# A Strassen-Winograd MLP kernel: one more nested product, accumulating stores and a new order of the weight sums

## The chip, the cores and the metric

The kernel runs on one core of one Trainium2 chip. The metric is device time in microseconds (us), the median of several executions. Executions of the kernel before agree within 0.2%. Engines are named as in the profile: PE is TensorE (matmul), DVE is VectorE, ACT is ScalarE, POOL is GpSimd, SP is SyncE, which issues most DMAs (in the kernel before 454 of 594 plain ones and all 54 transposes). bX, bY, bZ, bW and bT are the banks that PE writes its results into.

## The reference

```python
batch, m, k, h, n = 16, 512, 768, 3072, 768      # all float32

def reference(x, w1, b1, w2):
    y = np.matmul(x, w1) + b1
    y = 0.5 * y * (1.0 + erf(y / np.sqrt(2.0)))
    return np.matmul(y, w2)
```

The rows of x are handled in eight blocks of 1024. Each block has a first product (x with W1, then GELU) and a second product (with W2).

## The kernel before

Matmuls run in fp16 with fp32 accumulation. Both products use the Strassen-Winograd scheme: sums of blocks on DVE, then 7 block products instead of 8. Some of the seven W2 products go one level deeper and are again done as 7 instead of 8; I call these **nested**. Later blocks nest all seven; blocks 0 and 1 nest only some, and do the rest in plain **row units** (128 rows at a time, 12 matmuls of 384 columns for one product). Which ones are nested is one table of (block, product):

```python
HYBRID = ((0, 2), (1, 1), (1, 4), (1, 2))
```

A nested product needs sums of quarters of its W2 operand. They are made once by DVE in a few **staging buffers**, stored to a DRAM scratch `w2s` by SP, and loaded again where they are used:

```python
def split_w2(p, t, q=None):
    b11, b12, b21, b22 = quarters(p)
    def put(q, src, eng=nc.sync):
        eng.dma_start(out=w2s[p, q][:], in_=src)
    t = {n: spare[k] for n, k in zip((7, 5, 6, 4), t)}       # t: four staging buffers
    for n, a, b in ((7, b22, b12), (5, b12, b11), (6, b22, t[5]), (4, b21, t[6])):
        def f(n=n, a=a, b=b):
            tt(t[n], a, b, SUB)                              # DVE
            puts.append([LAG[0], lambda eng: put(n, t[n], eng)])   # stored LAG slots later, by SP
        later(WB, f, slow if q is None else q)
```

LAG is 2, and 3 in block 1's last row units. A sum that writes a staging buffer must wait until the last store out of that buffer has landed. In the kernel before, the order was: products 6, 1, 4, 2 in block 0's row units, 7 and 5 in the nested units of block 1 (buffers 6 to 9), and 3 in block 1's last row units (buffers 1 to 4).

The program places all side work in numbered slots of a unit's period. In block 0's first product two of these placements matter here:

```python
if slot == (1 if pos < at[1, 0] else 4) and pos + 1 < len(seq) and seq[pos + 1][0] == 0:
    prep_wt(seq[pos + 1][1])                 # DVE sums of the next W1 tile
if slot == 4:
    ...
    if pos == at[1, 0] - 2:
        x_sums(1, soon, slice(0, RH // 2), (0, 1))    # first-half sums of block 1's x
```

At the very start PE runs matmuls whose result nobody reads, while the inputs load (`spin(9)`, then four times `spin(2)`):

```python
def spin(n):
    for k in range(n):
        nc.tensor.matmul(out=(bX[1], bY[1])[k % 2][:], lhsT=zero[:, 0, 0:P], rhs=zero[:, 0, :],
                         start=True, stop=True, skip_group_check=True)
```

## Time and profile before

| | before |
|---|---|
| time, median of 3 | 852.22 us (851.93 to 852.35) |
| span of the profiled execution | 850.3 us |
| PE busy, matmuls | 843.9 us (99%), 6468 |
| last matmul starts | 846.31 us |
| from there to the end | 4.03 us |

PE is the bound and has hardly a gap. The list of PE's waits (engine, bank and line, released by; then us in total, times, longest) holds only the start-up:

```profile
PE bX L756 <- DVE arena L742: 1.2, 1, 1.2
PE bT L330 <- DVE arena L762: 1.1, 2, 0.9
```

The DMA view of the kernel before for 178 to 195 us (out<-in, issuing queue, count, size each, median us from issue to landing) shows stores of W2 sums landing far later than in a quiet stretch (3.9 us for those of 118 to 180 us):

```profile
w2s<-arena SPq DMA_DIRECT2D x5, 288.0 KB, 7.7
arena<-in_x_dram POOLq DMA_DIRECT2D x5, 192.0 KB, 7.9
```

### The profile page before, as it was taken

To read this page: it belongs to the slowest core of one execution; us is meant where nothing else is said; L and a number is where in the kernel's file an instruction comes from. 1 tells how busy PE (TensorE), PEld (TensorE's weight loads), DVE (VectorE), ACT (ScalarE), POOL (GpSimd) and SP (SyncE) were. 2 spreads that over 40 slices of the span, in tenths; PEclk is the share of its full clock that TensorE was granted. 3 is DMA by queue.
4 is the path that set the end of the run, shared out by engine and by line. 5 is a ranking of instruction groups with operands and counts; after the bars stand their busy time and mean duration, and the time that the engine had idled before them with its cause. 6 is when DMAs were issued, how large, how long until landed. Compare 5 with 4: busy or idle time off the path is not lost.

```text
span 850.3 us, 16583 instructions
## 1 busy us (share of the span) xinstructions
PE 843.9 (99%) x6468; PEld 571.3 (67%) x6468; DVE 671.1 (79%) x1132; ACT 423.6 (50%) x692; POOL 89.9 (11%) x147
## 2 busy tenths in 40 slices
PE   8999999999999999999999999999999999999998
PEld 5444445697544897449964499645995469944798
DVE  5766679877757998679976799667996689956998
ACT  4777762221277413773147822587216771277611
POOL 5021100022200002000020000200002100010000
PEclk9999999999999999999999999999999999999999
DMA  9998697679899699977999689995999949984398
GB/s 226 193 281 182 159 194 256 232 203 262 314 278 207 199 336 363 307 166 246 337 372 283 134 287 335 373 286 112 314 345 349 293 102 331 354 312 170 101 303 290
DMA packets 144066, 220.82 MB, mean 260 GB/s; under 512 B 61916, under 2 KB 84884, under 8 KB 143988
## 3 DMA queue, kind: packets, MB, share of 16 engines
q1 hardware_dynamic: 117536, 178.36, 67.0%
q0 software_dynamic: 26272, 41.30, 21.7%
q8 instruction: 50, 0.82, 0.4%
q14 instruction: 28, 0.23, 0.1%
q10 hardware_dynamic: 180, 0.11, 0.0%
HBM read 182.07 MB, written 47.87 MB: 270 GB/s over the span
## 4 chain that ended last, share of the span: by engine, by line
PE 98%; DMA 1%; ACT 0%; DVE 0%; SPq 0%; issue 0%; ACTq 0%
PE bY L411 21%; PE bY L516 15%; PE bX L411 14%; PE bX L516 10%; PE bW L411 7%; PE bZ L411 7%; PE bZ L516 5%; PE bW L516 5%; PE bY L456 5%; PE bZ L456 2%; PE bW L456 2%; PE bY L603 1%; PE bX L603 1%; PE bX L456 1%; DMA arena<-in_x_dram 1%; PE bX L778 0%
## 5 line engine op out<-in xcount | busy, mean ns | idle before, releaser
L208 DVE TENSOR_TENSOR arena<-arena 128x1536 f16<-128x1536 f16 (+6 forms) x634 | 405.9, 671 | 6.6 <-PE bW L456 1.0
L411 PEld LDWEIGHTS <-arena 128*128 128x128 f16 x1974 | 192.5, 98 | 224.3 <-issue 0.6
L516 PEld LDWEIGHTS <-arena 128*128 128x128 f16 x3528 | 292.1, 98 | 8.3 <-issue 0.4
L411 PE MATMUL bY<-arena 128*128 128x512 f16 x846 | 214.4, 379 | 0.1
L629 DVE TENSOR_TENSOR arena<-bY,arena 128x512 f32<-128x512 f32 (+1 forms) x102 | 69.4, 680 | 119.0 <-PE bY L411 91.9
L516 PE MATMUL bY<-arena 128*128 128x192 f16 x1500 | 138.3, 246 | 0.0
L411 PE MATMUL bX<-arena 128*128 128x512 f16 x564 | 138.2, 379 | 0.0
L622 ACT COPY bY<-bX 128x512 f32<-128x512 f32 (+1 forms) x144 | 79.1, 549 | 118.2 <-DVE arena L565 81.5
L427 ACT ACTIVATE arena<-arena,b1t 128x1024 f16<-128x1024 f32 x94 | 108.0, 1149 | 52.0 <-DVE arena L657 52.0
L642 ACT COPY arena<-bW 128x512 f32<-128x512 f32 (+1 forms) x148 | 81.5, 551 | 92.2 <-PE bW L516 44.3
L516 PE MATMUL bX<-arena 128*128 128x192 f16 x1020 | 93.1, 246 | 0.1
L657 DVE TENSOR_TENSOR arena<-bZ,arena 128x512 f32<-128x512 f32 (+1 forms) x102 | 69.2, 679 | 22.1 <-PE bZ L411 18.2
L411 PE MATMUL bZ<-arena 128*128 128x512 f16 x282 | 76.2, 379 | 0.0
L411 PE MATMUL bW<-arena 128*128 128x512 f16 x282 | 76.2, 379 | 0.0
L548 POOL DMA_DIRECT2D out_dram<-arena x42 | 30.5, 728 | 409.1 <-DVE arena L653 375.0
L432 ACT ACTIVATE arena<-bX,b1t 128x512 f16<-128x512 f32 x94 | 64.0, 681 | 10.5 <-PE bX L411 10.5
L673 ACT COPY bZ<-bY 128x512 f32<-128x512 f32 (+1 forms) x58 | 30.8, 532 | 75.6 <-PE bY L456 30.0
L456 PEld LDWEIGHTS <-arena 128*128 128x128 f16 x480 | 46.9, 98 | 31.0 <-issue 0.2
L432 ACT ACTIVATE arena<-bY,b1t 128x512 f16<-128x512 f32 x94 | 63.4, 674 | 0.0
L516 PE MATMUL bZ<-arena 128*128 128x192 f16 x504 | 48.5, 246 | 0.0
L516 PE MATMUL bW<-arena 128*128 128x192 f16 x504 | 48.4, 246 | 0.0
L316 POOL DMA_DIRECT2D arena<-in_x_dram x60 | 32.3, 546 | 152.3 <-DMA arena<-arena 142.0
(62 smaller groups left out, 413.9 us busy)
## 6 DMA issues: line engine op xcount, KB each, us to landing
arena<-w2s SPq DMA_DIRECT2D x300, 288.0 KB, 4.6
arena<-w1s SPq DMA_DIRECT2D x72, 672.0 KB, 7.0
out_dram<-arena POOLq DMA_DIRECT2D x46, 384.0 KB, 7.4
w2s<-arena SPq DMA_DIRECT2D x49, 288.0 KB, 4.1
arena<-in_x_dram POOLq DMA_DIRECT2D x60, 192.0 KB, 7.3
w1s<-arena SPq DMA_DIRECT2D x12, 672.0 KB, 6.1
arena<-in_w_dram POOLq DMA_DIRECT2D x17, 384.0 KB, 7.5
out_dram<-arena SPq DMA_DIRECT2D x9, 384.0 KB, 2.6
```

The source lines that it names most:

```text
L208: nc.vector.tensor_tensor(out=o, in0=a, in1=b, op=op)
L316: nc.gpsimd.dma_start(out=xhs[t], in_=xr[:, sb * 8 + t, :])
L411: nc.tensor.matmul(out=dst[:, 0:RH], lhsT=w1_op(self.wt, slot)[:, c, :], rhs=a[:, c, :], start=first and c == 0, stop=c == self.C - 1, ski ...
L427: nc.scalar.activation(out=self.G[1][:, hi, :, :], in_=self.tmp, func=GELU, bias=b1t[:, 2 * hi + 1:2 * hi + 2])
L432: nc.scalar.activation(out=self.G[0][:, hi, row, :], in_=bank[:, 0:RH], func=GELU, bias=b1t[:, 2 * hi:2 * hi + 1])
L456: nc.tensor.matmul(out=dst[:, 0:N2], lhsT=a, rhs=w[:, :, c, :], start=first and c == 0, stop=c == self.C - 1, skip_group_check=True)
L516: nc.tensor.matmul(out=dst[:, t * N4:(t + 1) * N4], lhsT=a, rhs=w[:, c, :], start=first and c == 0 and t == ts[0], stop=c == NQ - 1, skip_ ...
L622: nc.scalar.copy(out=bY[u.g % 2][:, 0:u.F], in_=bX[u.g % 2][:, 0:u.F])
L629: nc.vector.tensor_tensor(out=u.c22(), in0=bY[u.g % 2][:, 0:u.F], in1=w[:, 0:u.F], op=ADD)
L642: nc.scalar.copy(out=w[:, 0:u.F], in_=bW[:, 0:u.F])
L657: nc.vector.tensor_tensor(out=u.c12(), in0=bZ[:, 0:u.F], in1=w[:, 0:u.F], op=ADD)
L673: nc.scalar.copy(out=bZ[:, 0:u.F], in_=bY[u.g % 2][:, 0:u.F])
```

## The change

The intent: nest product 4 of block 0 too (fewer matmuls), let DMA add the results of block 0's products 2 and 4 into the output in memory instead of DVE and ACT, and move the sums of W1 tile 6 so that a bank is emptied in time. To make room, the W2 sums get a new order. The core of the diff:

```diff
-        HYBRID = ((0, 2), (1, 1), (1, 4), (1, 2))
+        HYBRID = ((0, 2), (0, 4), (1, 4), (1, 1), (1, 2))
...
             def finish(self):
-                if self.p == 2:
-                    for n in range(NU):
-                        nc.gpsimd.dma_start(out=orr[...], in_=self.dst[:, n // 2, n % 2])
+                if self.sb and self.p != 2:
+                    return
+                for n in range(NU):
+                    ...
+                    if self.sb:
+                        nc.gpsimd.dma_start(out=o, in_=d)
+                    else:
+                        nc.gpsimd.dma_start(out=o, in_=d, accum_op=ADD)
...
-            if slot == (1 if pos < at[1, 0] else 4) and pos + 1 < len(seq) and seq[pos + 1][0] == 0:
+            if slot == (1 if pos < at[1, 0] - 2 else 4) and pos + 1 < len(seq) and seq[pos + 1][0] == 0:
                 prep_wt(seq[pos + 1][1])
...
-                    for p, t in ((6, (0, 1, 2, 3)), (1, (4, 5, 0, 1)), (4, (2, 3, 4, 5)), (2, (0, 1, 2, 5))):
-                        split_w2(p, t)
+                    w4 = (6, 4, 5, 3)
+                    split_w2(4, w4, ns=(5, 6, 4))
+                    split_w2(1, (0, 1, 2, 6))
+                    split_w2(2, (3, 0, 1, 2))
+                    split_w2(4, w4, ns=(7,))
...
-                split_w2(7, (6, 7, 8, 9))
-                split_w2(5, (6, 7, 8, 9))
+            if m == 2 and slot == 5:
+                for p in (6, 7):
+                    split_w2(p, (7, 8, 9, 10))
...
             if k == 0 and slot == 4:
                 LAG[0] = 3
-                split_w2(3, (1, 2, 3, 4))
+                for p in (5, 3):
+                    split_w2(p, (0, 2, 3, 5))
```

Cut: the new places of buffers and level sums, full-row stores of block 0, and the changed slots of the W2 loads.

More of the change, by code (lines that the diff above doesn't have):

```diff
@@ L152 @@
     tmps1 = [tmp_at(o_tmp + 4 * k * RH) for k in range(2)]
-    o_stage = o_wt + 2 * N + PAR
+    o_stage = o_wt + PAR
     stage = [cut(o_stage + k * WB, WB, "p (c n) -> p c n", c=NQ)
@@ L164 @@
           for o in (o_x0 + W2_N, o_x0 + W2_N + GS_N, o_x1, o_x1 + GS_N)]
-    osbs = [[cut(o, n).bitcast(FP32) for o, n in zip(oo, (2 * N2, 2 * N))]
-            for oo in ((o_x1 + 2 * GS_N + 2 * N + 2 * N2, o_wt),
-                       (o_x1 + 2 * GS_N + 2 * N, o_x1 + 2 * GS_N))]
-    assert 2 * N + 4 * N2 <= PAR
-    par02, par1, par4 = [cut(o, PAR).bitcast(FP32).rearrange(
-        "p (r t h n) -> p r t h n", r=2, t=2, h=2) for o in (o_wt + 2 * N, 2 * XT_N, o_x1 + 2 * GS_N)]
+    osbs = [[cut(o + a * 2 * N, 2 * N).bitcast(FP32) for a in range(2)]
+            for o in (o_wt, o_x1 + 2 * GS_N)]
+    par02, par04, par1, par4 = [cut(o, PAR).bitcast(FP32).rearrange(
+        "p (r t h n) -> p r t h n", r=2, t=2, h=2)
+        for o in (o_wt, o_x1, 2 * XT_N, o_x1 + 2 * GS_N)]
     par11 = cut(o_w2, W2P).bitcast(FP32).rearrange("p (c n) -> p c n", c=NH)[:, 0:8, 0:N4].rearrange(
@@ L180, in wb_at @@
         return cut(off, WB, "p (c n) -> p c n", c=NQ)
-    hyb_lev = [[strip(0, 0, 0, 0), strip(1, 1, 0, 0), Gs[0][1][:, 0:NQ, 0, 2 * P:RH], strip(1, 1, NQ, 0)],
-               [strip(0, 1, 0, 0), strip(0, 0, NQ, 0), strip(0, 1, NQ, 0), strip(0, 0, 0, 2 * P)],
-               [strip(0, 1, 0, 2 * P), strip(0, 0, NQ, 2 * P), strip(0, 1, NQ, 2 * P), strip(0, 0, 0, 0)],
-               [strip(0, 1, 0, 0), strip(0, 0, NQ, 0), strip(0, 1, NQ, 0), strip(0, 0, NQ, 2 * P)]]
+    S = [strip(0, a, c, r) for r in (0, 2 * P) for c in (0, NQ) for a in range(2)]
+    hyb_lev = [[S[0], S[1], Gs[0][1][:, 0:NQ, 0, 2 * P:RH], S[2]],
+               [S[3], S[4], Gs[0][1][:, 0:NQ, 1, 2 * P:RH], S[6]],
+               [S[5], S[7], S[0], S[1]],
+               [S[2], S[3], S[4], S[6]],
+               [S[5], S[0], S[7], S[2]]]
     spare = stage + [wb_at(2 * XT_N + o) for o in
@@ L189 @@
     assert XT_N + 2 * WB + 5 * K == GR // 2
-    hyb_w = {2: {7: stage[0], 5: stage[1], 6: stage[2], 4: stage[5]},
-             1: dict(zip((7, 4, 5, 6), map(wb_at, (o_x0 + W2_N, o_x0 + W2_N + WB, o_x1, o_x1 + WB)))),
-             4: {7: wb_at(o_x1), 4: wb_at(o_x1 + WB), 5: stage[3], 6: stage[4]}}
+    w4 = {7: stage[6], 5: stage[4], 6: stage[5], 4: wb_at(o_x0 + W2_N)}
+    hyb_w = [{7: stage[3], 5: stage[0], 6: stage[1], 4: stage[2]}, w4, w4,
+             {7: stage[0], 5: stage[1], 6: stage[2], 4: stage[3]},
+             {7: stage[6], 5: stage[4], 6: stage[5], 4: stage[1]}]
     b1t = wp.tile([P, 2 * NH], FP32, name="b1t")
@@ L266, in quarters, with split_w2 @@
             return w[:, 0, 0:NQ, :], w[:, 1, 0:NQ, :], w[:, 0, NQ:NH, :], w[:, 1, NQ:NH, :]
-        def split_w2(p, t, q=None):
+        def split_w2(p, t, q=None, ns=(7, 5, 6, 4)):
             b11, b12, b21, b22 = quarters(p)
@@ L279, in f, with load_w2s @@
                     puts.append([LAG[0], lambda eng: put(n, t[n], eng)])
-                later(WB, f, slow if q is None else q)
-        def load_w2s(p, qs):
+                if n in ns:
+                    later(WB, f, slow if q is None else q)
+        def load_w2s(m, qs):
             for q in qs:
-                nc.sync.dma_start(out=hyb_w[p][q], in_=w2s[p, q][:])
+                nc.sync.dma_start(out=hyb_w[m][q], in_=w2s[HYBRID[m][1], q][:])
         def raw_w2(p):
@@ L357 @@
                    5: GA, 6: GB, 7: G1[:, :, 1, :]}
-        HYBRID = ((0, 2), (1, 1), (1, 4), (1, 2))
+        HYBRID = ((0, 2), (0, 4), (1, 4), (1, 1), (1, 2))
         def operand(sb, p):
-            return OPERAND[p] if sb else Gs[0][1][:, :, 0, :]
+            return OPERAND[p] if sb else Gs[0][1][:, :, p // 4, :]
         def half_sums(c, ks=(0, 1, 2)):
@@ L442, in __init__ @@
                 self.lean = sb > 0
-                self.eng = nc.gpsimd if self.lean else nc.sync
                 self.o = osbs1[u - NU] if self.lean else osbs[u % 2]
             def mm(self, p, dst, first, c0, c1):
-                if p == 2 or self.lean and p in (1, 4):
+                if p in (2, 4) or self.lean and p == 1:
                     return
@@ L452, in mm @@
                 for c in range(c0, c1):
-                    a = {1: G1[:, c, 0, r], 4: G2[:, c, 1, r],
-                         3: GS[3][:, c, :], 5: GS[0][:, c, :], 6: GS[1][:, c, :],
+                    a = {1: G1[:, c, 0, r], 3: GS[3][:, c, :], 5: GS[0][:, c, :], 6: GS[1][:, c, :],
                          7: GS[2][:, c, :]}[p]
@@ L466, in c12 @@
             def c12(self):
-                return self.o[0]
+                return self.o[0] if self.lean else self.o[0][:, N2:N]
             def c22(self):
@@ L472, in right_done @@
             def right_done(self):
-                self.eng.dma_start(out=orr[:, self.sb * 8 + self.u, N2:N], in_=self.o[0])
+                nc.gpsimd.dma_start(out=orr[:, self.sb * 8 + self.u, N2:N], in_=self.o[0]) if self.lean else \
+                    nc.sync.dma_start(out=orr[:, self.sb * 8 + self.u, :], in_=self.o[0])
             def left_done(self, row, bank):
-                if row == 0:
-                    if not self.lean:
-                        nc.scalar.copy(out=self.rows(par02), in_=bank[:, 0:N2])
+                if self.lean and row == 0:
                     return
@@ L482, in left_done @@
                 else:
-                    nc.scalar.copy(out=self.o[1][:, 0:N2], in_=bank[:, 0:N2])
-                self.eng.dma_start(out=orr[:, self.sb * 8 + NU + self.u, :], in_=self.o[1])
+                    nc.scalar.copy(out=self.o[row][:, 0:N2], in_=bank[:, 0:N2])
+                if row == 1:
+                    eng = nc.gpsimd if self.lean else nc.sync
+                    eng.dma_start(out=orr[:, self.sb * 8 + NU + self.u, :], in_=self.o[1])
         units3 = {}
@@ L586, in __init__ @@
                 self.g, (self.sb, self.p) = g, HYBRID[m]
-                self.lev, self.w = hyb_lev[m], dict(hyb_w[self.p])
+                self.lev, self.w = hyb_lev[m], dict(hyb_w[m])
                 b11, _, b21, b22 = quarters(self.p)
                 self.w.update({1: b11, 2: b21, 3: b22})
-                self.add = {0: par02, 1: par1}[self.sb] if self.p == 2 else None
-                self.dst = {1: par1, 4: par4, 2: par11}[self.p] if self.sb else par02
+                self.add = par1 if self.sb and self.p == 2 else None
+                self.dst = {(0, 2): par02, (0, 4): par04, (1, 1): par1, (1, 4): par4,
+                            (1, 2): par11}[self.sb, self.p]
                 self.alloc = lambda: None
@@ L608, in finish @@
             def finish(self):
-                if self.p == 2:
-                    for n in range(NU):
-                        nc.gpsimd.dma_start(
-                            out=orr[:, self.sb * 8 + n, 0:N2].rearrange("p (h n) -> p h n", h=2),
-                            in_=self.dst[:, n // 2, n % 2])
+                if self.sb and self.p != 2:
+                    return
+                for n in range(NU):
+                    o = orr[:, self.sb * 8 + self.p // 4 * NU + n, 0:N2].rearrange(
+                        "p (h n) -> p h n", h=2)
+                    d = self.dst[:, n // 2, n % 2]
+                    if self.sb:
+                        nc.gpsimd.dma_start(out=o, in_=d)
+                    else:
+                        nc.gpsimd.dma_start(out=o, in_=d, accum_op=ADD)
         def p1(u, c0, c1):
@@ L946, in fill_mm1, with drain @@
                 flush(soon)
-        def drain(slot, eng=nc.sync, wait=True):
+        def drain(slot, n=0, eng=nc.sync, wait=True):
             for f in puts:
@@ L952, in drain @@
                 puts.pop(0)[1](eng)
-            if slot > 1:
-                for f in raws[:2]:
-                    f()
-                del raws[:2]
+            for f in raws[:n]:
+                f()
+            del raws[:n]
         def fill_mm2_one(sb, U, slot):
@@ L967, in fill_mm2_one @@
                         raw_w2(p)
-                    for p, t in ((6, (0, 1, 2, 3)), (1, (4, 5, 0, 1)), (4, (2, 3, 4, 5)), (2, (0, 1, 2, 5))):
-                        split_w2(p, t)
-            drain(slot)
+                    w4 = (6, 4, 5, 3)
[3 more added lines that the diff above has]
+                    split_w2(4, w4, ns=(7,))
+            drain(slot, 3 if U == 0 and slot > 1 else 0)
             if slot == 2:
@@ L983, in fill_mm2_one @@
                 lev_sums(None, m=0, ks=(2,))
-            if U + 1 == NU and slot == 2:
-                lev_sums(None, m=1, ks=(0, 1, 2))
             if slot > 1:
@@ L996, in fill_hyb @@
         def fill_hyb(sb, m, slot):
-            drain(slot)
+            drain(slot, int(slot > 1))
             if m == 0 and slot == 1:
-                load_w2s(1, (7, 4))
-                lev_sums(None, m=1, ks=(3,))
-            if m == 0 and slot == 4:
-                load_w2s(1, (5, 6))
-            if m == 0 and slot == 5:
-                lev_sums(None, m=2)
-            if m == 1 and slot == 5:
-                lev_sums(None, m=3, ks=(0, 1))
-            if m == 1 and slot == 6:
-                split_w2(7, (6, 7, 8, 9))
-                split_w2(5, (6, 7, 8, 9))
-            if (m, slot) in ((1, 6), (2, 1), (2, 3), (2, 5), (3, 1), (3, 5)):
-                slow.pop(0)[1]()
-            if m == 2 and slot == 1:
-                load_w2s(4, (7, 4))
-                lev_sums(None, m=3, ks=(2,))
-            if m == 2 and slot == 5:
-                lev_sums(None, m=3, ks=(3,))
-            if m == 3 and slot == 2:
+                load_w2s(1, (4,))
+                lev_sums(None, m=1)
+            if m == 0 and slot == 6:
+                lev_sums(None, m=2)
+            if m == 2 and slot == 1:
+                load_w2s(3, (5, 6, 7, 4))
+                lev_sums(None, m=3, ks=(0, 1, 2))
+            if m == 2 and slot == 4:
+                lev_sums(None, m=3, ks=(3,))
+            if m == 3 and slot == 1:
+                load_w2s(4, (5, 6, 7))
+                lev_sums(None, m=4, ks=(0, 1, 2))
+            if m == 3 and slot == 4:
+                lev_sums(None, m=4, ks=(3,))
+            if m == 4 and slot == 1:
+                load_w2s(4, (4,))
+            if m == 2 and slot == 5:
+                for p in (6, 7):
+                    split_w2(p, (7, 8, 9, 10))
+            if slow and (m == 2 or slot in (1, 4, 6)):
+                slow.pop(0)[1]()
+            if m == 4 and slot == 2:
                 for k in (0, 1):
@@ L1023, in fill_hyb @@
                 flush(queue)
-                if m == 1:
+                if m == 2:
                     load_next_x(2, range(5))
-                if m == 3:
+                if m == 4:
                     for t in range(3):
```

## The prediction

> **What bounds the kernel now.** I read the page first: its head, the busy shares and the chain that ended last. TensorE (PE) is busy 99% of the span, and the chain of waits is PE for 98%.
>
> ```profile
> span 850.3 us, 16583 instructions
> ...
> PE 843.9 (99%) x6468; PEld 571.3 (67%) x6468; DVE 671.1 (79%) x1132; ACT 423.6 (50%) x692; POOL 89.9 (11%) x147
> ...
> PE 98%; DMA 1%; ACT 0%; DVE 0%; SPq 0%; issue 0%; ACTq 0%
> ```
>
> So only two things can move the time: the matmul work itself, and a new or removed gap on PE. I then read the chain in order of time at the two places the change touches. The first is around 38 us, in the first product, where the chain leaves PE for once. The columns are start, length, piece.
>
> ```profile
> 38.52 0.71 DVE bZ L675
> 39.22 0.04 issue
> 39.27 0.81 PE bY L411 x3
> ```
>
> PE waits there for VectorE's (DVE's) copy of bank bY to bZ. The timeline of PE shows what it cost. Two neighbouring periods begin with the same six bX matmuls, followed by three bY matmuls:
>
> ```profile
> 32.82 1.46 PE L411 MATMUL bX<-arena 128*128 128x512 f16 x6
> ...
> 34.12 0.81 PE L411 MATMUL bY<-arena 128*128 128x512 f16 x3
> ...
> 37.69 1.46 PE L411 MATMUL bX<-arena 128*128 128x512 f16 x6
> ...
> 39.27 0.81 PE L411 MATMUL bY<-arena 128*128 128x512 f16 x3
> ```
>
> From bX to bY it is 1.30 us in the undisturbed period and 1.58 us in the second. The gap is 0.28 us. The timeline of DVE (start, length, idle before it and releaser) tells why:
>
> ```profile
> 35.04 0.69 DVE L629 TENSOR_TENSOR arena<-bY,arena 128x512 f32<-128x512 f32 x1 [0.87 <-PE bY L411]
> 36.67 1.14 DVE L208 TENSOR_TENSOR arena<-arena 128x384 f16<-128x384 f16 x3 [0.94 <-DMA arena<-in_w_dram]
> 37.73 0.68 DVE L657 TENSOR_TENSOR arena<-bZ,arena 128x512 f32<-128x512 f32 x1
> 38.51 0.70 DVE L675 COPY bZ<-bY 128x512 f32<-128x512 f32 x1
> 39.12 1.41 DVE L208 TENSOR_TENSOR arena<-arena 128x384 f16<-128x384 f16 x3
> ```
>
> DVE stood 0.94 us for the load of W1 tile 6, and the bank eviction (L657) and the copy (L675) queued behind it. This is what the second part of the change aims at. In the order of instructions the row at 39.12 is the fourth sum of tile 6 and then the two first-half sums of the next block's transposed x (128x768 each).
>
> The second place is block 0's second product. The chain there is PE without a gap. A full-width product is 12 matmuls in 1.95 us; a product of the nested level (L603) is 12 in 0.99 us:
>
> ```profile
> 159.69 3.90 PE bY L456 x24
> 163.59 0.99 PE bX L603 x12
> ...
> 172.41 1.98 PE bX L603 x24
> ```
>
> [...] an eviction whose bank was ready waited behind sums that waited for a load. [...] the trace of before shows a granted clock of 1.00 in the stretches I read from the span's start to 336 us[...]. [...] each accumulating store waits for the landing of the plain store of its rows. No accumulating DMA is in the trace of before.
>
> **The change, part 1: product 4 at the nested level.** It takes away product 4 of the four row units of block 0, 4 x 12 = 48 matmuls of 384 columns, 4 x 1.95 = 7.80 us of PE. It adds seven sub-products of 24/2 = 12 matmuls of 192 columns, 7 x 0.99 = 6.93 us. All of it is on the path: 6.93 - 7.80 = **-0.87 us**.
>
> What comes beside it: four level sums on DVE (about 0.95 us each), but product 2's four adds of a partial result (0.55 us each) turn into ScalarE copies (0.48 us), since DMA now adds; DVE gains some 1.6 us, ScalarE 4 us. GpSimd issues four stores more, at 0.64 us each. Stores grow by four of 192 KB (full rows) plus the four new ones. The busy shares leave room on average:
>
> ```profile
> 140.00:160.00 20.00, 20.00 (x125) 12.04 (x123) 17.57 (x25) 4.07 (x9) 0.00 (x0) 1.00 0.90 324
> ...
> 172.00:195.00 23.00, 23.00 (x279) 22.85 (x278) 17.44 (x26) 6.63 (x14) 4.87 (x9) 1.00 0.87 219
> ```
>
> (columns: stretch and its length, then busy PE, weight load, DVE, ScalarE, GpSimd, clock, DMA share, GB/s.) But a unit period shrinks from 6 x 1.95 = 11.7 us to 9.75, so I placed the DVE queue of the changed program against PE's order. The tightest place is the seam of the two nested units of block 0. Unit 3's last eviction can start 0.99 + 1.95 + 0.99 + 1.95 = 5.88 us (+0.16 pipeline) into the first one's period. Behind it stand six level sums: three at a pitch of 0.77 us (three independent ones took 2.48 us: (2.48 - 0.95)/2), three at the full 0.95, as each reads its forerunner; with 0.47 for the eviction this is 0.47 + 2.31 + 2.85 = 5.63. DVE is free at 11.67; the period is 4 x 0.99 + 2 x 1.95 = 7.86 long, so 3.81 us into the next. The eviction that PE then needs takes 0.56, done at 4.37; PE needs the bank after five sub-products, at 4.95. It fits by about 0.6 us. I found no other deadline closer, and expect no gap. The reordered W2 sums write staging buffers again some 7 us after they were filled; their stores need about 4.1 us to land (DMA issues, w2s), and a short DVE wait there has most of a period of slack.
>
> **Part 2: tile 6's sums later.** The sums leave slot 1 of period 5 for slot 4, behind the copy to bZ. If nothing took their place, this would give back the 0.28 us. But the changed order of DVE shows what stands in that slot instead: the two first-half sums of block 1's x, which in the kernel before stood behind the copy. The first of them waits for two DMA transposes, and the later of these (the fourth in the queue) is told of in the view of the transposes' line, cut to its issue:
>
> ```profile
> L322 SPq DMA_TRANSPOSE arena<-arena x1: 2927/2927/2927, 32.3 to 32.3; - x1
> ...
> DMA to landing us min/median/max: 6.7/6.7/6.7
> ```
>
> It lands at 32.3 + 6.7 = 39.0 us. Before, that sum came up about 39.4 and did not wait. Now it heads the queue at 35.7 and holds DVE until 39.0. From there: first sum 0.58 (the second reads it), second 0.56 less 0.08 of overlap gives the eviction at 40.06; the copy 0.78 later (37.73 to 38.51) at 40.84; PE 0.76 after the copy's start (38.51 to 39.27), at 41.60. Before it was 39.27: **+2.33 us**. The sums of tile 6 then run just ahead of the product that uses the second of them (it is ready about 42.2, PE wants it at 41.60 + 0.65 = 42.25): up to 0.1 us more. The later periods keep their distances, since their inputs follow PE. PE has no later wait in which the shift could vanish, so it goes whole into the end.
>
> **Sum.** 852.22 - 0.87 + 2.33 + 0.05 = **853.7 us**: slower by 0.2%, the small saving more than eaten by a worse wait for another DMA.
>
> **Rivals.** (a) The change works as meant: tile 6's wait vanishes, the transposes land earlier than I read, or the wait fits in slack. 852.22 - 0.87 - 0.28 = 851.1. For it: the intent, and that no DVE wait on a transpose is in the trace of before. Against: the landing at 39.0 and the order of the queue. (b) The nested part makes its own gap: the seam of 0.6 us slips, or a staging buffer's store lands late; DMA is busy 0.87 to 0.90 there. I put 0.3 to 1 us on it, so about 854.5 on top of part 2. (c) The PE gap of some 2.6 us lets the clock fall[...]. (d) The accumulating stores are slow and hold up the sums that reuse their buffer. The first such sum stands about 16 us after the issue; a plain store of this size lands in 4.0 us, so even a tripling is hidden.
>
> **Range and chances.** I give my reading of part 2 some 85%, with half a microsecond either way for the landing; rival (a) 10%; (b) and (c) stretch the upper side. The range is 852.6 to 855.2. Two per cent is 17 us, which no rival reaches: within 2% 0.99, slower 0.008, faster 0.002.
>
> **What would show it.** PE: 36 matmuls more, and the second product of block 0 shorter by 0.87 us from its first full-width product to the first of block 1's nested ones. DVE: a wait of about 3.3 us near 35.7 to 39.0 put down to a DMA of the arena (transposes), with the W1 wait gone; PE's gap before bY near 39 to 41.6, about 2.6 us instead of 0.28. The prediction is wrong if that wait is absent or short, if PE shows gaps between 120 and 195 us, or if the granted clock dips.

## The result, and the profile after

The changed kernel took **860.56 us** (858.67 to 863.47, 6 runs) against 851.91 us (851.56 to 852.35, 6 runs) for the kernel before in the same rounds, a ratio of 1.0103 with a 95% interval of 1.0081 to 1.0125. Ratios here are the mean time of one kernel's fast runs over that of the other's of the same rounds, so not quite the ratio of the medians that I quote. It is 1% slower, which still counts as "the same" at 2%, but 5.4 us above the predicted range.

The page of the changed kernel:

```profile
span 860.4 us, 16683 instructions
...
PE 845.7 (98%) x6504; PEld 574.8 (67%) x6504; DVE 673.4 (78%) x1134; ACT 426.5 (50%) x700; POOL 95.6 (11%) x151
```

There are 36 matmuls more, as foreseen, and PE's busy time rose by 1.8 us although the work shrank. So idle time was added, and part of the work ran slower. PE's waits name the idle time:

```profile
PE bY L457 <- ACT bZ L681: 3.0, 1, 3.0
PE bY L606 <- DVE bZ L678: 3.0, 1, 3.0
PE bX L764 <- DVE arena L750: 1.2, 1, 1.2
PE bY L414 <- DVE bZ L683: 1.1, 1, 1.1
PE bY L414 <- ACT bZ L681: 0.5, 1, 0.5
```

The third is the start-up, as before. The other four are new.

**Gap A, at 40 us (the first product).** DVE's timeline of the changed kernel (start, length, what; in brackets the idle time before it and its releaser):

```profile
37.55 1.15 DVE L210 TENSOR_TENSOR arena<-arena 128x768 f16<-128x768 f16 x2 [1.95 <-DMA arena<-arena]
38.62 0.68 DVE L665 TENSOR_TENSOR arena<-bZ,arena 128x512 f32<-128x512 f32 x1
39.41 0.70 DVE L683 COPY bZ<-bY 128x512 f32<-128x512 f32 x1
```

The two x sums now head the queue, wait 1.95 us for a DMA transpose, and the eviction and the copy queue behind them. This is the mechanism that I predicted. The size is not: the transpose landed at 37.46 and let the sum start at 37.55, not at 39.0. PE's next bY matmuls started at 40.16 in place of 39.27.

**Gap B, at 197 us (block 1's nested units).** DVE again:

```profile
193.23 0.76 DVE L210 TENSOR_TENSOR arena<-arena 128x1152 f16<-128x1152 f16 x1 [3.30 <-DMA w2s<-arena]
193.90 0.55 DVE L654 TENSOR_TENSOR arena<-bW,arena 128x384 f32<-128x384 f32 x1
...
196.57 0.56 DVE L678 TENSOR_TENSOR bZ<-bY,arena 128x384 f32<-128x384 f32 x1
```

The row at 193.23 is a W2 sum: quarter 5 of product 7. It overwrites the staging buffer of quarter 5 of product 6. The buffer had been filled by 181.5, and product 7's sum came to it 8.5 us later. Its store was issued by SP at 183.96 and landed 9.2 us later (DMA view for 184.01 to 184.11 us):

```profile
w2s<-arena SPq DMA_DIRECT2D x1, 288.0 KB, 9.2
```

DVE stood 3.30 us for it, the evictions came late, and PE waited 2.96 us for the add at 196.57.

**Gap C, at 233 us (block 1's last row units)** is the same again, twice, with product 3's sums over product 5's buffers:

```profile
225.78 0.76 DVE L210 TENSOR_TENSOR arena<-arena 128x1152 f16<-128x1152 f16 x1 [2.27 <-DMA w2s<-arena]
...
231.10 0.76 DVE L210 TENSOR_TENSOR arena<-arena 128x1152 f16<-128x1152 f16 x1 [3.22 <-DMA w2s<-arena]
```

Here the buffers had been filled 16 and 15 us before product 3's sums came to them (at 223.5 and 227.9). But the store of the first had been issued only at 219.19, although its sum was done by about 207: the program puts it three slots behind the sum, and SP issued x transposes from 206.9 to 219. The store of the second was issued 8.7 us after its sum and took 9.5 us to land. DVE's list of waits sums the three up; no such line is in the list of before:

```profile
DVE arena L210 <- DMA w2s<-arena: 8.8, 3, 3.3
```

**Why the stores were slow.** The DMA view of the changed kernel for the same 178 to 195 us:

```profile
w2s<-arena SPq DMA_DIRECT2D x6, 288.0 KB, 9.2
arena<-w2s SPq DMA_DIRECT2D x4, 288.0 KB, 9.0
arena<-in_x_dram POOLq DMA_DIRECT2D x5, 192.0 KB, 12.2
```

Against before there is one W2 store more, there are three W2 loads more and three transposes fewer in this stretch; 4.33 MB moved in place of 4.00. Which of these slows the stores no run separates. But the stage was crowded before too (7.7 us), and buffers were shared before too: product 5 took over product 7's. Its second sum ran at 193.92, 10.3 us after the buffer had been filled and 1.9 us after its store had landed (in 8.3 us). The new order came 8.5 us after the filling, and so ahead of the landing.

**The clock.** After gap B, PE ran at half clock. The windows view of the changed kernel, cut where the granted clock changed (197.62 and 201.03) and else in stretches of that same length (stretch, its length, PE busy, then other engines; the third number from the end is the granted clock):

```profile
194.21:197.62 3.41, 0.45 (x7) 0.44 (x6) 3.41 (x6) 0.48 (x1) 0.00 (x0) 1.00 1.10 313
197.62:201.03 3.41, 3.41 (x17) 2.18 (x15) 2.72 (x5) 0.00 (x0) 0.00 (x0) 0.50 0.87 236
201.03:204.45 3.42, 3.42 (x29) 2.44 (x28) 2.38 (x3) 0.48 (x1) 1.07 (x2) 1.00 0.89 141
228.34:231.75 3.41, 1.58 (x9) 0.75 (x8) 0.65 (x1) 0.00 (x0) 0.00 (x0) 1.00 1.01 406
231.75:235.17 3.42, 2.25 (x14) 1.35 (x14) 3.42 (x6) 1.02 (x2) 0.89 (x2) 1.00 1.02 304
```

In the second row 3.41 us passed at 0.50, which loses half of that, 1.7 us (my estimate, from these two numbers). Gap C (3.16 us) is as long as gap B (3.12 us) and left the clock alone: it lies across the last two rows, and the granted clock was 1.00 from 201.03 to the last matmul. In these two rows PE was busy 1.58 and 2.25 us, in the first row, just ahead of the half clock, 0.45 us. Why the clock fell after one gap and not after the other was not shown.

**The books.** From the start times of matmuls in PE's timelines:

| stretch | before | after | difference |
|---|---|---|---|
| start to the first W1 product in Strassen form | 21.49 | 21.37 | -0.12 |
| to block 0's second product | 99.04 | 100.06 | +1.02 (gap A) |
| to block 1's first nested matmul | 55.68 | 54.80 | -0.88 (fewer matmuls) |
| to block 2's second product | 104.53 | 113.08 | +8.55 (B, C, clock) |
| to the last matmul | 565.57 | 565.43 | -0.14 |
| from the last matmul to the end | 4.03 | 5.70 | +1.67 |
| span | 850.34 | 860.44 | +10.10 |

The +8.55 is made of gap B, 3.12, gap C, 3.16 + 0.70 (start to start of neighbouring matmuls, less what this takes without a wait), and 1.7 for the clock: 8.7; the difference of 0.1 I did not trace. The last row but one was a surprise: the end of the program, which the change does not touch, got longer by 1.67 us. The DMA view of the last stores, before (844.6 to 850 us):

```profile
out_dram<-arena SPq DMA_DIRECT2D x1, 384.0 KB, 2.5
out_dram<-arena SPq DMA_DIRECT2D x1, 192.0 KB, 2.4
...
out_dram<-arena ACTq DMA_DIRECT2D x1, 96.0 KB, 2.3
```

and after (853 to 859.5 us):

```profile
q8 instruction: 1, 0.02, 1.1%
...
out_dram<-arena SPq DMA_DIRECT2D x1, 384.0 KB, 4.2
out_dram<-arena SPq DMA_DIRECT2D x1, 192.0 KB, 4.0
out_dram<-arena ACTq DMA_DIRECT2D x1, 96.0 KB, 3.3
```

The same stores take 1.0 to 1.7 us longer, and a queue is there that moves instructions, not data. More on this under e9.

### The profile page after: what moved, and what is told of

Read it like the earlier page. It is cut to its first block, busy times and chain, and to the rows that moved or that the text cites. A ratio compares the mean times of both kernels' runs of the same rounds, so it can differ in the third digit from the quotient of the medians.

```text
span 860.4 us, 16683 instructions
## 1 busy us (share of the span) xinstructions
PE 845.7 (98%) x6504; PEld 574.8 (67%) x6504; DVE 673.4 (78%) x1134; ACT 426.5 (50%) x700; POOL 95.6 (11%) x151
## 4 chain that ended last, share of the span: by engine, by line
PE 71%; ACT 0%; DVE 0%; issue 0%; ACTq 0%
PE bY L414 16%; PE bY L518 14%; PE bX L414 11%; PE bX L518 10%; PE bZ L414 5%; PE bW L414 5%; PE bZ L518 5%; PE bW L518 5%; ACT bZ L681 0%; DVE arena L210 0%; ACTq L681 0%
## 5 line engine op out<-in xcount | busy, mean ns | idle before, releaser
L210 DVE TENSOR_TENSOR arena<-arena 128x1536 f16<-128x1536 f16 (+6 forms) x638 | 410.0, 673 | 17.5 <-DMA w2s<-arena 8.8
```

Of the source, the lines that this page charges most:

```text
L210: nc.vector.tensor_tensor(out=o, in0=a, in1=b, op=op)
```

## The experiments

My theory after the result: gap A is part 2 of the change; gaps B and C come from staging buffers used again before their stores have landed; the half clock follows from gap B. Rival: the accumulating stores are slow by nature and clog the DMA queues.

### e1 and e2: part 2 undone, and part 2 alone

e1 is the changed kernel with tile 6's sums back in slot 1; e2 is the kernel before with the move alone.

```diff
-            if slot == (1 if pos < at[1, 0] - 2 else 4) and pos + 1 < len(seq) ...     # e1, in the changed kernel
+            if slot == (1 if pos < at[1, 0] else 4) and pos + 1 < len(seq) ...
```

> The changed kernel with only the sums of W1 tile 6 put back to slot 1. Theory (three separate gaps on PE): the gap before bY near 40 us falls from 1.3 us to about 0.3 us, as in the kernel before, the two later gaps (3.1 us near 197, 3.2 and 0.7 us near 233 to 240) stay, so the time falls by 1.0 us, to about 859.5 with the spread of the changed kernel (858.7 to 863.5). Rival (one cause): the early delay shifts TensorE against the DMA queues and makes the later gaps too; then they vanish with it and the time comes to about 851.

> The kernel before with only the sums of tile 6 moved to slot 4. Theory of the prediction: DVE heads its queue with the first-half x sums and waits for a DMA transpose, PE's gap near 40 us grows from 0.28 us to 1.3 us (landing as in the changed kernel's profile) or 2.6 us (landing at 39.0 us as in the profile before), no later gap; 853.0 to 854.3 us. Rival (the move works as intended): the gap of 0.28 us vanishes, 851.6 us.

Measured: e1 858.34 us (857.23 to 859.92), ratio 1.0076 [1.0061, 1.0091] to before, 852.0 in these rounds. e2 853.34 us (853.13 to 857.11), ratio 1.0027 [1.0006, 1.0047]. In e2 the stretch from the first W1 product to block 0's second product was 99.87 us, 0.83 more than before; in e1 it was 98.84. DVE's timeline of e2 shows the wait that the move brings:

```profile
37.74 1.15 DVE L208 TENSOR_TENSOR arena<-arena 128x768 f16<-128x768 f16 x2 [1.76 <-DMA arena<-arena]
...
39.59 0.70 DVE L675 COPY bZ<-bY 128x512 f32<-128x512 f32 x1
```

So part 2 costs about 1 us, by the way that I predicted, and is only a small part of the loss. (One of e2's four runs, 857.11 us at a clock of 0.998, is 4 us above the others. No trace of it was kept, and its cause stays open.) e1 had gap B at 4.32 us with 6.83 us at half clock, and gap C at only 0.35 us: where the landings fall differs from run to run, which fits the scatter of these kernels by several microseconds.

### e3, e4, e5: buffers of their own for the second set of sums

If reuse is the cause, another buffer takes the wait away without touching the work. e3 was a first try for gap C, e5 the mended one; e4 does it for gap B. Not every sum gets a new buffer: in e4 the third and fourth sum of product 7 still take buffers of product 6 (the first and second), and in e5 the fourth of product 3 takes the second of product 5.

```diff
-                for p in (6, 7):                       # e4: gap B
-                    split_w2(p, (7, 8, 9, 10))
+                split_w2(6, (7, 8, 9, 10))
+                split_w2(7, (11, 12, 7, 8))            # 11, 12: the place of block 0's product-2 results
...
-                for p in (5, 3):                       # e5: gap C
-                    split_w2(p, (0, 2, 3, 5))
+                split_w2(5, (0, 2, 3, 5))
+                split_w2(3, (1, 4, 6, 2))              # e3: (1, 4, 6, 0)
```

> The changed kernel, but in block 1's four last row units the sums of product 3 write other staging buffers (1, 4, 6, 0) than those of product 5 (0, 2, 3, 5). Theory: the DVE waits of 2.3 and 3.2 us for stores of w2s near 226 and 231 us vanish, with them PE's gaps of 3.2 and 0.7 us, and the time falls by 3.9 us, to about 856.7; the gap near 197 us stays. Rival (DVE is simply overloaded there, or the transposes hold everything): PE keeps a gap of over 1 us between 225 and 241 us.

> The changed kernel, but the sums of product 7 in the nested units write two buffers that the accumulating stores have left (and two of product 6's, third and fourth) instead of all four of product 6's. Theory: the DVE wait of 3.3 us for a store of w2s near 190 to 193 us vanishes, with it PE's gap of 3.1 us near 197 us and the stretch of 3.41 us at half clock that followed it (1.7 us); the time falls by about 4.8 us, to about 855.8. Rival (accumulating stores clog the DMA rings and something else waits as long): PE keeps a gap of over 1 us between 185 and 200 us.

> As the failed run before it, but the fourth sum of product 3 goes to buffer 2 (buffer 0 is under a W1 load that stands ahead of that sum in program order, which made the result wrong). Theory: no DVE wait for a store of w2s after 220 us, PE's gaps near 233 and 240 us together below 0.5 us, the gap near 197 us (3 to 4.5 us, with 3.4 or 6.8 us at half clock) stays; 856 to 858 us. Rival (DVE overloaded there): a PE gap over 1 us between 225 and 241 us.

**e3 was my mistake.** Buffer 0 shares its place with a W1 tile whose late load stands ahead of that sum, so the result was wrong (relative error 0.233) and new waits for the load arose: 864.35 us (859.17 to 866.04). Nothing follows from its time.

**e4**: 857.06 us (855.46 to 862.66), ratio 1.0059 [1.0042, 1.0076]. Gap B is gone. In its profile, which is its slowest run, gap C was 3.32 us, a wait for a W1 load added 1.92 us just ahead, and the half clock moved to that place (6.83 us from 229.53):

```profile
PE bY L457 <- ACT bZ L681: 3.2, 1, 3.2
...
PE bX L414 <- DMA arena<-w1s: 1.8, 1, 1.8
```

**e5**: 859.8 us (858.2 to 861.33), ratio 1.0094 [1.008, 1.0109] to 852.13. Gap C is gone, B is there with 3.29 us:

```profile
PE bY L606 <- DVE bZ L678: 3.1, 1, 3.1
PE bX L764 <- DVE arena L750: 1.2, 1, 1.2
PE bY L414 <- DVE bZ L683: 1.1, 1, 1.1
```

In its profile each mend takes away its own gap and no other. One profile alone would not settle C, which was only 0.35 us in e1 and is absent in e11 below, with the buffers still shared. The waits of DVE for stores of `w2s` settle it: at B such a wait stands in all six profiles with shared buffers (after, e1, e3, e5, e6, e11) and in none of the seven without; at C in all five with (after, e1, e4, e6, e11) and in none of the eight without. The shared buffers, used again so soon, are the cause of B and C. The times fell less than expected: e5's median by 0.8 us and not by some 3, e4's by 3.5 and not by 4.8. In the profiles C is the shorter the longer B is (after 3.12 and 3.86 us, e6 4.31 and 2.51, e1 4.32 and 0.35, e11 5.10 and none), so that a mend of C gains little where B is long. This may be why; it is not shown for the runs without a profile.

### e6: the accumulating stores made plain

```diff
-                        nc.gpsimd.dma_start(out=o, in_=d, accum_op=ADD)
+                        nc.gpsimd.dma_start(out=o, in_=d)
```

The result is wrong on purpose (relative error 0.30); the bytes written and the issues stay.

> The changed kernel with the eight accumulating stores issued as plain stores: the result is wrong on purpose, the transfers are the same in number and place, only the addition in memory is gone. Theory (buffers reused behind a loaded DMA queue; the five x loads and three w2s loads do the loading): the store of w2s that the gap near 197 us waits for still takes 8 us or more to land and the gap stays over 2 us; time as the changed kernel, 858 to 863 us. Rival (the addition in memory slows the queue): that store lands in 4 to 6 us, the gap near 197 us falls below 1 us, and the time comes to 856 us or less.

Measured: 861.25 us (859.58 to 862.9), ratio 1.0106 [1.0093, 1.012], with gap B at 4.3 us and C at 1.82 + 0.69. The store that gap B waits for took 10.8 us to land. The addition in memory is not the cause, and the rival falls.

### e7 and e8: all mended

e7 joins e1, e4 and e5. e8 has e4 and e5, keeps tile 6's sums in slot 4, and moves the first-half x sums behind the copy in the same slot:

```diff
+            if slot == 4 and pos == at[1, 0] - 2:              # e8: now after the eviction and the copy
+                x_sums(1, soon, slice(0, RH // 2), (0, 1))
...
-                if pos == at[1, 0] - 2:
-                    x_sums(1, soon, slice(0, RH // 2), (0, 1))
```

> The changed kernel with all three mended: tile 6's sums back in slot 1, product 7's and product 3's sums in buffers of their own. Theory: PE's gaps are those of the kernel before (0.3 us near 39 us) and what is left is the smaller product: 0.87 us below before, about 851.1 us. Rival (nested product 4 costs more than its matmuls save, by waits of its own): 852 us or more, with a PE gap between 120 and 200 us.

> As the run before it, but tile 6's sums and the first-half x sums both stand behind the copy to bZ in slot 4. Theory: the gap near 39 us is gone too, another 0.28 us: about 850.8 us. Rival: the six sums behind the copy delay the next eviction and a gap of as much comes one period later; 851.1 us or more.

Measured: e7 852.89 us (852.34 to 854.94), ratio 1.0014 [1.0002, 1.0026]; e8 852.44 us (852.19 to 856.91), ratio 1.0012 [0.9997, 1.0027]. The 8 us are gone. PE's list of waits in e8 has only the start-up left; DVE does not stand ahead of the copy any more, in contrast to gap A:

```profile
36.13 0.69 DVE L665 TENSOR_TENSOR arena<-bZ,arena 128x512 f32<-128x512 f32 x1 [0.87 <-PE bZ L414]
36.93 0.70 DVE L683 COPY bZ<-bY 128x512 f32<-128x512 f32 x1
```

But I had expected a gain over before. In e8 the last matmul starts at 844.65, 1.66 us sooner than before (0.46 of it because the first W1 product happened to start sooner), and the end comes at the same time: the tail was 5.65 us. It was 5.29 to 5.80 in each of the profiles of the changed kernel and of e1, e3, e4, e5, e6, e7 and e8, and 4.03 and 4.05 in before and e2. Neither the addition (e6) nor part 2 (e1, e2) makes it.

### e9, e10, e11: the length of PE's program

The DMA records hold fetches of 16 KB in a queue of kind "instruction". Their number fits PE: in the changed kernel there are 51 for 2 x 6504 matmuls and weight loads, one for 255 instructions, in the kernel before 50 for 2 x 6468, one for 259. That they bring PE's program is my reading of these counts. In before and e2 the last fetch starts 8.0 and 9.0 us ahead of the last matmul. In the eight profiles with the long tail one starts 0.3 to 0.6 us ahead of it and holds one DMA engine for about 1 us (1.15 us in after), amid the last stores. These eight have 36 matmuls more (72 instructions with their weight loads), and I take it that these moved a fetch there. That it holds the stores up by taking a DMA engine from them is an inference. To test whether its place matters, I changed the length of PE's program where it does no harm: start-up matmuls, whose result is thrown away, are cut into four narrow ones.

```diff
             for k in range(n):
-                nc.tensor.matmul(out=(bX[1], bY[1])[k % 2][:], lhsT=zero[:, 0, 0:P], rhs=zero[:, 0, :], ...)
+                parts = 4 if len(spun) < 12 else 1          # e9 (kernel before): 36 more; e10, e11: 17, 51 more
+                spun.append(k)
+                w = RH // parts
+                for j in range(parts):
+                    nc.tensor.matmul(out=(bX[1], bY[1])[k % 2][:, j * w:(j + 1) * w],
+                                     lhsT=zero[:, 0, 0:P], rhs=zero[:, 0, j * w:(j + 1) * w], ...)
```

> The kernel before with twelve of its 128x512 start-up matmuls (their result is thrown away) cut into four 128x128 ones: 36 matmuls and 36 weight loads more in TensorE's program, the same columns of work, nothing else changed. Theory (program length): the profile shows TensorE's program being fetched in pieces of 16 KB, one every 10.7 us near the end; before, the last such fetch starts 8.0 us ahead of the last matmul; in all seven kernels with product 4 nested, which also have 36 matmuls more, it starts 0.3 to 0.6 us ahead of it, takes about 1 us of one DMA engine, and that engine's packets of the last stores come 1.2 us or more late. So here [...] one more should start at about -0.4 us, and the time from the last matmul's start to the end should go from 4.03 to about 5.7 us: the time 852.1 to 853.7 (+1.2 to +1.7). Rival (the tail comes from product 4, its staging or its store order): 852.1, tail 4.0.

> The mended changed kernel (both part 2 sums behind the copy, staging buffers of their own) with all 17 start-up matmuls cut into four: 51 matmuls more at the start. Theory (program length): the fetch that starts 0.4 us ahead of the last matmul moves forward [...] and is over when the last stores go out; the next would be due after the end. Tail 5.65 to about 4.0 us, time 852.4 to about 850.9, which would beat the kernel before by 1.2 us (ratio 0.9986). Rival: tail stays at 5.6 and the time at 852.4.

> The changed kernel itself with the same 51 more start-up matmuls. If the program-length theory holds for the changed kernel as it was, its tail falls from 5.70 to about 4.0 us and its time by 1.2 to 1.7 us, to about 859; the three gaps and the half-clock stretch stay. Rival: 860.5 as it was, tail 5.7.

**e9**, the kernel before with 36 matmuls more: 853.55 us (853.15 to 853.84) against 852.01, ratio 1.0018 [1.0005, 1.003]. A fetch now starts 0.76 us ahead of the last matmul, the tail grew from 4.03 to 5.12 us, and the last stores take nearly as long as in the changed kernel (844.6 to 851 us):

```profile
q8 instruction: 1, 0.02, 1.1%
...
out_dram<-arena SPq DMA_DIRECT2D x1, 384.0 KB, 3.7
out_dram<-arena SPq DMA_DIRECT2D x1, 192.0 KB, 3.8
```

This is 1.09 us of the 1.5; the profile also has a gap of 0.99 us at 39 us in place of 0.28.

**e10**, e8 with 51 more: the fetch moved to 6.1 us ahead of the last matmul (an estimate gives 4.7: 102 instructions more, at 255 for one fetch and 10.7 us from fetch to fetch, the mean of the last three steps in after, move it by 4.3 from 0.4) and the tail fell from 5.65 to 4.01 us, as the theory says:

```profile
out_dram<-arena SPq DMA_DIRECT2D x1, 384.0 KB, 2.5
out_dram<-arena SPq DMA_DIRECT2D x1, 192.0 KB, 2.3
```

**e11**, the changed kernel with 51 more: tail 4.00 us in place of 5.70. So the position of the fetch is what makes the tail long or short, in both directions. The times are less kind. e10 took 852.46 us (ratio 1.0005 [0.9993, 1.0018]), not 850.9, and e11 860.1 (859.93 to 863.5). In e10's profile the first W1 product started at 22.54 us, 1.5 us later than in e8. In e11's, gap B had grown to 5.1 us while C was gone.

### e12: part 2 alone, mended

This is the kernel before with e8's order of tile 6's sums and the x sums.

> The kernel before with part 2 alone in a mended form: the sums of W1 tile 6 and the first-half x sums both in the later slot, behind the copy that empties the bank. Theory: the copy no longer stands behind the wait for the transposes in VectorE's queue, so the excess of 0.28 us at 39 us goes: 851.8, between 851.6 and 852.2. Rival: moving the x sums later makes their own reader wait, over 852.5 with a new gap after 41 us. It also tells how much of a mended version's gain is owed to nesting product 4.

Measured: 851.7 us (851.5 to 852.19), ratio 0.9997 [0.9983, 1.0011]. The gap at 39 us is gone: the stretch from the first W1 product to block 0's second product is 98.77 us, 0.27 less than before. The median lies where it was expected, but five rounds do not tell it from before.

### e13, e14, e15: does a version beat both kernels?

e13 is e8 with 36 start-up matmuls more, e14 is e8 again, and e15 is e10 again, all on one chip.

> The mended version with twelve of its start-up matmuls cut into four, so 36 matmuls more. Program length: the fetch moves [...] before the last stores go out. Tail 5.65 to about 4.0 us. If the late start of e10 was the landing of its input loads, the start is as in e8 (21.0 +- 0.7 us) and the time goes to 850.6 to 851.4, below e8 of these rounds by 1.0 to 1.6 us and below before by about 1. If more start-up matmuls hold up the start, it is later by about 1 us and the time is that of e8.

> The mended version as it ran in e8, for the same rounds and chip: 852.4, the program fetch 0.4 us ahead of the last matmul, tail 5.65 us.

> The mended version with 51 more start-up matmuls as in e10, again. If the late start of e10 was chance: start 21.0 +- 0.7 us, tail 4.0, time about 851. If the 51 matmuls cause it: start again at about 22.5 us, and 852.4.

| | time (range) | ratio to before (851.83) | first W1 product | tail |
|---|---|---|---|---|
| e13 | 852.41 (850.68 to 852.54) | 1.0001 [0.9989, 1.0014] | 21.46 | 4.00 |
| e14 | 852.35 (852.26 to 852.71) | 1.0006 [0.9993, 1.0018] | 21.08 | 5.68 |
| e15 | 851.98 (851.41 to 852.98) | 1.0003 [0.999, 1.0017] | 21.79 | 4.01 |

The tail behaved as expected in all three. In e10, e13 and e15 the start was later by 0.4 to 1.5 us than in e8 and e14, with waits of PE for x loads. Over the twelve profiles without extra matmuls the start lies between 20.77 and 22.22 us, and with 36 more it was 20.63 (e9) and 21.46, so for these chance is enough. The three with 51 more (e10, e11, e15: 22.54, 22.19 and 21.79) all started later than eleven of the twelve. So 51 may well cost something at the start, by the matmuls themselves or by the moved fetch (at 12 to 13.5 us, amid the input loads, instead of about 19); three profiles do not show it, and no run separates the two. e13's profile, which is its slowest run, also shows that the nested stage has little to spare: a W2 load came 1.5 us late at 191 us.

```profile
PE bY L606 <- DMA arena<-w2s: 1.5, 1, 1.5
```

No version is faster than the kernel before by more than its interval. The lowest single time is e13's 850.68 us.

## Why the prediction was wrong

By its own steps:

- **Part 1, -0.87 us: right.** The stretch that holds it went from 55.68 to 54.80 us, -0.88, and stayed at 54.80 or 54.81 in every profile with product 4 nested. PE had no gap between 120 and 190 us in the changed kernel; the seam that I computed with 0.6 us to spare held.
- **Part 2, +2.33 us: right in mechanism, too large.** The mis-sized term is the landing of the fourth transpose, 39.0 us. I read it rightly in the trace of before (issued at 32.33, landed at 39.06), but took for granted that it stays there. With the sums moved it was issued at 31.71 and landed at 37.46 us (e2: 31.77 and 37.65); with them put back in e1 it landed at 38.98 again. Why it comes sooner stays open. The books show +1.02 (e2: +0.83).
- **The step that failed** is this one: "The reordered W2 sums write staging buffers again some 7 us after they were filled; their stores need about 4.1 us to land, and a short DVE wait there has most of a period of slack." The time until a buffer is used again was not the fault: it was 8.5 us at gap B and 15 to 16 at gap C. The landing was: the stores of this stage landed after 9 us, and even before the change after 7.7 us. A term was missing: the time from the sum to the issue of its store, 2.5 us at gap B and 12 and 8.7 us at gap C. And the slack was not there: DVE waits of 2.3 to 3.3 us became PE waits of 3.0 us, twice. e4 and e5 take the waits away one by one, and e7 and e8 both. That is about 7 us, and rival (b), which named this very store, had 0.3 to 1 us for it.
- **Rival (c), the clock, judged unlikely: it happened**, at another gap. After gap B of 3.12 us, 3.41 us passed at a granted clock of 0.50, a loss of 1.7 us by my estimate. (No trace of before shows a lower clock. Its time lay even outside of the range that it was said to stretch.)
- **Rival (d), slow accumulation: refuted** (e6).
- **Not thought of:** +1.67 us at the end of the program, from a program fetch that the 36 added matmuls moved among the last stores (e9, e10, e11).

The sum: 852.12 (the profiled run of before) - 0.88 + 1.02 + 8.55 + 1.67, with -0.26 for the start and the later blocks, is 862.2; the profiled run of after took 862.3. With all mended (e8), -0.88 and the vanished 0.28 at 39 us are eaten by the longer tail (+1.62 in its profile, beside a start that came 0.46 sooner), and the time is that of before.

## What to carry to other kernels

When a buffer that a DMA empties is used again, take the landing time from the same stage and the same queue, not from the program's median, count the wait of the issuing engine's queue too, and follow the waiting instruction to the evictions behind it. Look at the granted clock after each wait of TensorE: here 3.12 us (gap B) was followed by 3.41 us at 0.50, an estimated 1.7 us on top, and 3.16 us (gap C) was not; in the seven profiles with half clock amid the matmuls (after, e1, e3, e4, e5, e6, e11) it lasted 3.41 or 6.83 us. And after adding or removing many matmuls look at the end of the trace: the time from the last matmul to the end was 5.12 to 5.80 us with a program fetch 0.3 to 0.8 us ahead of that matmul, and 4.00 to 4.05 us with none so near. Throw-away matmuls at the start moved it (here without a gain in time that is clear of noise).
